# The SSD output weight's first half kept in the dead columns of the normalised input

## The chip, the cores and the metric

The kernel runs on one core of one Trainium2 chip. The metric is the device time of one execution in microseconds (us), and the number that stands for a kernel is the median of several executions. A second number is used for the working: the span of one profiled execution, from its first to its last instruction.

## The reference, cut to what matters

One inference step of a two-layer decoder trunk. Layer 0 is a Mamba-2 state space mixer (SSD), layer 1 is latent attention (MLA); 1024 prompt tokens and 8 x 8 sample tokens use the same weights. Only the end of layer 0 matters here:

```python
y = y.reshape(b, t, SSD_D_INNER) * jax.nn.silu(z.astype(F32))
yg = y.reshape(b, t, SSD_GROUPS, SSD_D_INNER // SSD_GROUPS)
yg = yg * lax.rsqrt(jnp.mean(yg * yg, axis=-1, keepdims=True) + NORM_EPS)
y = yg.reshape(b, t, SSD_D_INNER) * norm_w.astype(F32)
out = jnp.einsum('bte,ed->btd', y.astype(h.dtype), w_out)
```

`z` is the gate: the normalised input times the first 2048 columns of `ssd_w_in`. `w_out` is 2048 x 1024 in float32. The result is added to the input rows and becomes the input of layer 1.

## The kernel before, in words

Tokens come in nine tiles: eight of 128 prompt tokens and one of 64 sample tokens. The 32 SSD heads come in eight groups of four. Every float32 operand of a large product is held as two halves, `hi` (rounded to the matmul's input format) and `lo` (the rest), and a product is three matmuls: hi*hi, hi*lo, lo*hi. Making the halves is one ACT instruction (`hi`) and one DVE or POOL instruction (`lo`).

The normalised input lies transposed in `xh` and `xl`, `[128, 8, 1152]` and `[128, 8, 1088]`: partition is input channel, the middle index its block of 128, the last index the token. For each group g, `Group.steps` makes 21 steps: 12 projections of convolution channels (line 88), then `gates`, nine steps, one for each token tile i, in which `mm_tok` (line 100) projects tile i with the columns `i*128 : i*128+128` of `xh` and `xl` as weights (tile names `pz`, then ACT copies the result to `z`, line 514). The scan of group g (`ssd_scan`, 13 pieces) is interleaved with the steps of group g+1. PSUM tiles tagged `pj` (two buffers) carry all projections.

After the steps of the last group 7, `left.close()` frees the pools on the left side of the on-chip memory (`wp` with the input weights, `rp`, `xT` with `xh` and `xl`, `al`). Only then `load_wout` (lines 709 to 720) brings in the first eight 128-row blocks of `w_out` into new tiles `woh` and `wol`: a 512 KB DMA into `wraw` (two buffers), an ACT instruction that multiplies with the norm weight and rounds (line 718), a DVE instruction for the rest (line 719). They lie where the freed pools were. Then the scan of group 7 runs, interleaved with pass "a" of `ssd_outproj`: for each token tile a load of four groups' rows (`yta`, line 734), a scaling on DVE (line 736), eight PE transposes (`ytpa`, line 746), their halves (`yha`, `yla`), and two half tiles of 24 matmuls each of 512 columns (`poa`, line 100), added to `xra` on DVE (line 755). The number of pieces of pass "a" that have been made after a weight `w` of the scan's 21 is `int((w - CA) * PAR)`, at most 17, with `CA = 4` and `PAR = 0.7`. What is left of the 18 pieces comes after the scan, beside the load of the second eight blocks; then comes pass "b" (`pob`) with them, then layer 1, whose first gate weights (`wgh`, `wgl`) and `ckv` weights (`ck0h` to `ck7l`) are loaded while pass "b" runs.

The program's text does not fix the order on each engine: at build time a scheduler orders the instructions of each engine, and each DMA queue, from a modelled timeline. On the chip every engine executes its own list strictly in that order, each instruction after waiting for what it needs. Almost all DMAs are issued by SP, in one such list.

Of the kernel before, what the change touches and what calls it, by code (L numbers as in the profile page):

```python
# [8 lines left out]
F32 = mybir.dt.float32  # L9
F32R = mybir.dt.float32r  # L10
AF = mybir.ActivationFunctionType
ALU = mybir.AluOpType
# [41 lines left out]
WORD = (0, 4, 6, 1, 2, 3, 5, 7)  # L54
NWA = 8
NR0 = 13
CA = 4
PAR = 0.7
YHB = {"ya": 2, "yb": 1}
XDB = 2  # L60
YB = 2
# [29 lines left out]
def mm_tok(nc, p, m, n, terms):  # L91
    ops = []
    for j, (a, b, a2, wh, wl) in enumerate(terms):
        if m == 64:
            x = [(p[:64, :n], a, wl), (p[:, :n], a2, wh)]
            ops += x if j else x[::-1]
        else:
            ops += [(p[:m, :n], *ab) for ab in ((a, wh), (a, wl), (b, wh))]
    for j, (o, a, b) in enumerate(ops):
        nc.tensor.matmul(o, a, b, start=(j == 0), stop=(j == len(ops) - 1))  # L100
        yield
# [604 lines left out]
    return load  # L706


def load_wout(k, pool, raws, kks, ws):
    nc = k.nc  # L710
    wo = k.I["ssd_w_out"][0]
    for kk in kks:
        hi = pool.tile([128, D], F32R, name=f"woh{kk}")
        lo = pool.tile([128, D], F32R, name=f"wol{kk}")
        raw = load_raw(raws, 1, D)[:, 0]
        nc.sync.dma_start(raw, wo[kk * 128 : kk * 128 + 128])
        nw = k.ssdn[:, kk : kk + 1]
        nc.scalar.activation(hi, raw, AF.Copy, scale=nw)
        nc.vector.scalar_tensor_tensor(lo, raw, nw, hi.bitcast(F32), op0=ALU.mult, op1=ALU.subtract)
        ws.append((hi, lo))  # L720


def ssd_outproj(k, ypools, ws, psum, k0, load, order, tag):
    nc = k.nc
    nk = len(ws)
    g0, ng = k0 // 2, nk // 2
    rs = k.cs.tile([128, 9, ng], F32, name="yrs" + tag)
    rstd_of(k, rs, k.yssq[:, :, g0 : g0 + ng], 256)
    for j, i in enumerate(order):
        t0, m = TILES[i]  # L730
        yp = ypools[j]
        nb = YHB[yp.name]
        y = yp.tile([128, ng, 256], F32, tag="yt", name=f"yt{tag}{i}", bufs=1)
        nc.sync.dma_start(y[:m].rearrange("p g c -> p (g c)"),
                          k.y_d[t0 : t0 + m, k0 * 128 : (k0 + nk) * 128])
        nc.vector.tensor_tensor(y[:m], y[:m], rs[:m, i].unsqueeze(2).to_broadcast([m, ng, 256]), op=ALU.mult)
        xr = yp.tile([128, D], F32, tag="xr", name=f"xr{tag}{i}", bufs=nb)
        load(xr, i)
        yh = yp.tile([128, nk, 128], F32R, tag="yh", name=f"yh{tag}{i}", bufs=nb)
        yl = yp.tile([128, nk, 128], F32R, tag="yl", name=f"yl{tag}{i}", bufs=nb)  # L740
        yv = y.rearrange("p g c -> p (g c)")
        for q in range(nk // 4):
            p = psum.tile([128, 512], F32, tag="tr", name=f"ytp{tag}{i}{q}", bufs=PB["tr"])
            for a in range(4):
                b = q * 4 + a
                nc.tensor.transpose(p[:, a * 128 : a * 128 + m], yv[:m, b * 128 : b * 128 + 128], k.ident[:m, :m])
            pv = p.rearrange("p (a t) -> p a t", a=4)[:, :, :m]
            qs = slice(q * 4, q * 4 + 4)
            split(k, yh[:, qs, :m], yh[:, qs, 64:] if m == 64 else yl[:, qs], pv)
        for hf in range(2):  # L750
            c = slice(hf * 512, hf * 512 + 512)
            p = psum.tile([128, 512], F32, tag="pj", name=f"po{tag}{i}{hf}", bufs=PB["pj"])
            drain(mm_tok(nc, p, m, 512, [(yh[:, kk, :m], yl[:, kk], yh[:, kk], ws[kk][0][:, c], ws[kk][1][:, c])
                                         for kk in range(nk)]))
            nc.vector.tensor_tensor(xr[:m, c], xr[:m, c], p[:m], op=ALU.add)
            if m == 64:
                nc.vector.tensor_tensor(xr[:m, c], xr[:m, c], p[64:], op=ALU.add)
            if hf == 0:
                yield
        (nc.gpsimd if k0 and i > 6 else nc.sync).dma_start(k.h_d[t0 : t0 + m], xr[:m])  # L760
        yield
# [6 lines left out]
def layer_ssd(k):  # L768
    tc, nc = k.tc, k.nc
    k.h0 = ExitStack()  # L770
    PB.update(PB1)
    stc = ExitStack()
    k.cs = stc.enter_context(open_pool(tc, name="cs", bufs=1))
    ssd_tiles(k)
    k.y_d = k.dram.tile([T, DIN], F32, name="y_d")
    k.h_d = k.dram.tile([T, D], F32, name="h_d")
    with ExitStack() as st:
        psum = st.enter_context(open_pool(tc, name="ps1", bufs=2, space=PS))
        left, right = ExitStack(), ExitStack()
        wp = left.enter_context(open_pool(tc, name="wp", bufs=2))  # L780
        rp = left.enter_context(open_pool(tc, name="rp", bufs=2))
        xp = left.enter_context(open_pool(tc, name="xT", bufs=1))
        k.xh = xp.tile([128, 8, T + 64], F32R, name="xh")
        k.xl = xp.tile([128, 8, T], F32R, name="xl")
        al = left.enter_context(open_pool(tc, name="al", bufs=1))
        gp = right.enter_context(open_pool(tc, name="gp", bufs=1, side="right"))
        pools = (wp, rp, gp, psum, (al, gp))
        g0 = Group(k, 0, pools)
        st0 = g0.steps()
        with open_pool(tc, name="x0", bufs=1, side="right") as p0:  # L790
            g0.raws[1] = p0

            k.sqp = lambda name: gp.tile([128, 5, 256], F32, tag="z", name=name, bufs=3).rearrange(
                "p a c -> p (a c)")[:, :D]

            def before():
                load_vectors(k, p0, psum)
                for bi in range(2):
                    g0.pre[bi] = g0.weights(bi)

            def after():
                ssd_consts(k)
                conv_state_T(k, p0, psum)

            norm_steps(k, x_loader(k), None, k.xh, k.xl, p0, psum, [st0], XB, before, after)
        for _ in range(6):
            next(st0)
        with open_pool(tc, name="zd", bufs=1, side="right") as p0:
            load_zdt(k, p0)
            for _ in st0:  # L810
                pass
            ssd_dt(k, p0, psum)
        sp = right.enter_context(open_pool(tc, name="sp", bufs=2, side="right"))
        k.cblk = [sp.tile([128, 4, 64], F32R, name=f"cblk{q}") for q in range(2)]
        for t in k.cblk:
            nc.gpsimd.memset(t.bitcast(F32), 0.0)
        gr = g0
        for g in range(G - 1):
            nx = Group(k, g + 1, pools)
            steps = nx.steps()  # L820
            done = 0
            w = 0
            for x in ssd_scan(k, gr, (sp, psum)):
                w += x
                while done < int(w + 0.01):
                    next(steps, None)
                    done += 1
            for _ in steps:
                pass
            gr = nx  # L830
        left.close()
        wsa, wsb = [], []
        wa = st.enter_context(open_pool(tc, name="woa", bufs=1))
        ya = st.enter_context(open_pool(tc, name="ya", bufs=1))
        load_wout(k, wa, wa, range(NWA), wsa)
        pa = ssd_outproj(k, (ya,) * 9, wsa, psum, 0, x_loader(k), range(9), "a")
        w, done = 0, 0
        for x in ssd_scan(k, gr, (sp, psum)):
            w += x
            while done < min(int((w - CA) * PAR), 17):  # L840
                next(pa)
                done += 1
        right.close()
        h0 = k.h0.enter_context(open_pool(tc, name="h0", bufs=1, side="right"))
        k.h0p = h0
        k.xt0 = [h0.tile([128, D], F32, tag="xt", name=f"xt{j}", bufs=3) for j in range(3)]
        k.sqp = lambda name: k.tok.rearrange("p i a h -> p (i a h)")[:, :D]
        yb = st.enter_context(open_pool(tc, name="yb", bufs=1, side="right"))
        wb = st.enter_context(open_pool(tc, name="wob", bufs=1, side="right"))
        load_wout(k, wb, wa, range(NWA, 16), wsb)  # L850
        for _ in pa:
            pass
        for j, _ in enumerate(ssd_outproj(k, YORD(yb, ya), wsb, psum, NWA, h_loader(k), range(9), "b")):
            if j == NR0:
                k.rows0 = norm_rows(k, 0, h_loader(k), h0, 3, k.xt0)
    stc.close()
# [452 lines left out]
def drain(g):  # L1309
    for _ in g:  # L1310
        pass
# [603 lines left out]
```

## Time and profile before

| what | us |
|---|---|
| median of three runs | 2028.72 (2023.08 to 2029.69) |
| the profiled execution, whole | 2021.9 |
| its span | 2020.1 |
| last gate projection on PE starts | 816.82 |
| first matmul of pass "a" starts | 835.35 |
| first matmul of pass "b" starts | 975.13 |

The page of the profile gives busy time by engine, the span in 40 slices (a digit is the busy share in tenths, and `PEclk` the granted TensorE clock in tenths of full speed), and groups of instructions. The views quoted below are: stretches of the span with each engine's busy time; the instructions of one engine in order of time (start, duration, engine, line, operation, tiles, count, and in brackets the idle time ahead of it with what ended it); and groups of equal instructions (line, engine, operation, tiles, shape, count | busy time, mean ns of one | idle time ahead).

### The profile page before, as it was taken

The numbers are of one execution on the slowest core, as the hardware profiler recorded it, in microseconds if no ns is written. First come the engines' busy times: TensorE is split into PE (matmuls) and PEld (weight loads), VectorE is DVE, ScalarE is ACT, GpSimd is POOL, SyncE is SP. The second block draws the span as 40 slices with busy tenths as digits, with TensorE's granted clock in tenths as the row PEclk, the third lists the DMA queues.
The fourth block names the chain that finished last, engine by engine and source line by source line (L and its number), as shares of the span: only waits on it lengthen the run. The fifth ranks groups of instructions, "written<-read, shape, count | busy, mean of one in ns | idle before, by whom it ended". The sixth has DMA issues, their size and how long they took to land. (4 is left out here: it accounts for less than half of the span.)

```text
span 2020.1 us, 33410 instructions
## 1 busy us (share of the span) xinstructions
PE 1920.7 (95%) x12001; PEld 1744.5 (86%) x12001; DVE 1223.7 (61%) x2459; ACT 1107.6 (55%) x2535; POOL 788.6 (39%) x979
## 2 busy tenths in 40 slices
PE   6999999999999999899998999999999999799998
PEld 5899999999999999787777998898888887688887
DVE  4547566656566666755334314567787877866675
ACT  5456667666666666632114314435676777655552
POOL 1327555555655545631000001103343334755551
PEclk9999999999999999799999999999999999999999
DMA  4213323332333332645534432232121112554541
GB/s 149 57 51 93 90 86 92 82 97 82 93 82 96 85 97 66 214 141 193 167 120 138 129 147 76 73 104 65 49 66 39 50 39 78 167 170 135 148 146 37
DMA packets 182461, 206.59 MB, mean 102 GB/s; under 512 B 18988, under 2 KB 147896, under 8 KB 181912
## 3 DMA queue, kind: packets, MB, share of 16 engines
q1 hardware_dynamic: 177240, 184.67, 30.7%
q0 software_dynamic: 4976, 19.66, 3.2%
q8 instruction: 95, 1.56, 0.3%
q14 instruction: 70, 0.57, 0.1%
q10 hardware_dynamic: 80, 0.13, 0.0%
HBM read 151.10 MB, written 53.28 MB: 101 GB/s over the span
## 5 line engine op out<-in xcount | busy, mean ns | idle before, releaser
L88 PE MATMUL pj<-xh,wih 128*128 128x384 f32 (+1 forms) x768 | 256.5, 338 | 9.5 <-ACT xh L239 5.2
L88 PE MATMUL pj<-xl,wih 128*128 128x384 f32 (+1 forms) x768 | 255.4, 333 | 0.0
L88 PE MATMUL pj<-xh,wil 128*128 128x384 f32 (+1 forms) x768 | 255.0, 332 | 0.0
L474 DVE SCALAR_TENSOR_TENSOR acc<-raw,vec,acc 128x1112 f32<-128x1112 f32 x96 | 141.5, 1478 | 25.5 <-ACT acc L471 24.6
L88 PEld LDWEIGHTS pj<-xh,wih 128*128 128x128 f32 x768 | 145.8, 191 | 11.8 <-ACT xh L239 6.2
L1274 POOL TENSOR_TENSOR tl<-P,th 128x384 fp32r<-128x384 f32 (+1 forms) x96 | 91.0, 948 | 164.9 <-ACT P L1272 134.8
L88 PEld LDWEIGHTS pj<-xl,wih 128*128 128x128 f32 x768 | 146.3, 191 | 0.9
L88 PEld LDWEIGHTS pj<-xh,wil 128*128 128x128 f32 x768 | 146.1, 190 | 0.4
L100 PE MATMUL pz<-wih,xh 128*128 128x256 f32 x504 | 142.5, 286 | 0.0
L100 PE MATMUL pz<-wil,xh 128*128 128x256 f32 (+1 forms) x504 | 140.2, 284 | 0.0
L1271 ACT ACTIVATE th<-st 128x512 fp32r<-128x512 f32 x192 | 94.2, 490 | 65.2 <-PE st L1267 42.8
L100 PE MATMUL pz<-wih,xl 128*128 128x256 f32 x448 | 128.3, 286 | 0.0
L577 ACT ACTIVATE M<-M,tok 128x128 f32<-128x128 f32 (+1 forms) x288 | 90.5, 386 | 66.7 <-DVE M L574 66.5
L1563 POOL TENSOR_TENSOR kvl<-pgr,kvh 128x1024 fp32r<-128x1024 f32 x32 | 78.2, 2445 | 66.9 <-ACT kvh L1562 66.9
L100 PEld LDWEIGHTS pz<-wih,xh 128*128 128x128 f32 x504 | 95.8, 190 | 0.3
L1272 ACT ACTIVATE P<-st 128x512 f32<-128x512 f32 x192 | 93.3, 486 | 0.0
L100 PEld LDWEIGHTS pz<-wil,xh 128*128 128x128 f32 (+1 forms) x504 | 92.7, 184 | 0.8
L574 DVE TENSOR_TENSOR M<-M,negu 128x512 f32<-128x512 f32 x64 | 50.6, 791 | 68.7 <-DMA M<-acs_d 68.4
L130 DVE TENSOR_TENSOR wil<-wraw,wih 128x512 fp32r<-128x512 f32 x88 | 72.3, 829 | 30.2 <-ACT wih L129 28.8
L100 PEld LDWEIGHTS pz<-wih,xl 128*128 128x128 f32 x448 | 85.2, 190 | 0.1
L1274 DVE TENSOR_TENSOR tl<-P,th 128x512 fp32r<-128x512 f32 x96 | 72.0, 750 | 21.3 <-ACT P L1272 21.1
L560 POOL TENSOR_TENSOR xdd<-xsT,tok 128x256 f32<-128x256 f32 x64 | 49.6, 775 | 73.0 <-ACT xsT L546 72.7
(818 smaller groups left out, 6327.3 us busy)
## 6 DMA issues: line engine op xcount, KB each, us to landing
wraw<-in_ssd_w_in SPq DMA_DIRECT2D x92, 256.0 KB
M<-acs_d SPq DMA_DIRECT2D x64, 256.0 KB
s<-in_state_ssm SPq DMA_DIRECT2D x32, 256.0 KB
y_d<-y SPq DMA_DIRECT2D x64, 128.0 KB
out_s_ssm<-s SPq DMA_DIRECT2D x32, 256.0 KB
wraw<-in_ssd_w_out SPq DMA_DIRECT2D x16, 512.0 KB
q_d<-qt SPq DMA_DIRECT2D x32, 192.0 KB
qp<-q_d SPq DMA_DIRECT2D x8, 768.0 KB
```

What stands on the lines that cost most here:

```text
L88: nc.tensor.matmul(out, a, b, start=(i == 0), stop=(i == n - 1))
L100: nc.tensor.matmul(o, a, b, start=(j == 0), stop=(j == len(ops) - 1))
L130: (eng or nc.vector).tensor_tensor(lo, src, hi.bitcast(F32), op=ALU.subtract)
L474: nc.vector.scalar_tensor_tensor(acc, raw[:, j : j + n], k.convw[j][:, blk : blk + 1], acc, op0=ALU.mult, op1=ALU.add)
L560: nc.gpsimd.tensor_tensor(v3(xdd), v3(xsT), hb(2), op=ALU.mult)
L574: nc.vector.tensor_tensor(M[:m, :, :m], M[:m, :, :m], (k.negs if smp else k.negu)[:m, :m].unsqueeze(1).to_broadcast([m, 4, m]), op=ALU.add)
L577: nc.scalar.activation(M[:m, h, :m], M[:m, h, :m], AF.Exp, bias=tk[:, 0, 4 * g + h : 4 * g + h + 1])
L1271: nc.scalar.activation(th[:, :n], ps[:, :n], AF.Exp, scale=SCALE)
L1272: nc.scalar.activation(P[:, :n], ps[:, :n], AF.Exp, scale=SCALE)
L1274: eng.tensor_tensor(tl[:, :n], P[:, :n], th[:, :n].bitcast(F32), op=ALU.subtract)
L1563: nc.gpsimd.tensor_tensor(rl, raw, rh.bitcast(F32), op=ALU.subtract)
```

## The change: what it does, and the diff

Three edits belong together. The first eight blocks of `w_out` get no tiles of their own: block kk's halves are written into columns `kk*128 : kk*128+128` of all eight channel blocks of `xh` and `xl` (`wout_cols`), 8 x 128 values in each partition, and read from there as 4 x 128 columns by the matmuls of pass "a". Token tile kk's columns are dead once the last group's gate projection of tile kk is done. So `last_steps` issues blocks 0 to 3 inside the steps of group 7, ahead of steps 13, 15, 17 and 19 (gate projections of tiles 1, 3, 5 and 7 by index), with `rp`'s `raw` buffers for the raw rows; blocks 4 to 7 follow after `left.close()` with two raw buffers in a new small pool `wor`. Pool `xT` moves out of the group of pools that `left.close()` frees, so `xh` and `xl` stay, and all pools that are opened later lie elsewhere than before. `CA` goes from 4 to 1 and `PAR` from 0.7 to 0.6, so pass "a" starts earlier in the scan, at a lower rate: int(17 x 0.7) = 11 pieces within the scan before, int(20 x 0.6) = 12 now. The buffer that holds the descriptors of DMAs issued by POOL (the page gathers of layer 1 above all) is set to 4096 bytes.

```diff
-CA = 4
-PAR = 0.7
+CA = 1
+PAR = 0.6
+WCOLS = (13, 15, 17, 19)
...
+def wout_halves(k, kk, raw, hi, lo):
+    nc = k.nc
+    nw = k.ssdn[:, kk : kk + 1]
+    nc.scalar.activation(hi, raw, AF.Copy, scale=nw)
+    nc.vector.scalar_tensor_tensor(lo, raw, nw, hi.bitcast(F32), op0=ALU.mult, op1=ALU.subtract)
+
+
+def wout_cols(k, kk, raw, ws):
+    k.nc.sync.dma_start(raw, k.I["ssd_w_out"][0][kk * 128 : kk * 128 + 128])
+    cs = slice(kk * 128, kk * 128 + 128)
+    hi, lo = k.xh[:, :, cs], k.xl[:, :, cs]
+    wout_halves(k, kk, raw.rearrange("p (k e) -> p k e", k=8), hi, lo)
+    ws.append((hi, lo))
+
+
+def last_steps(k, steps, rp, ws):
+    for n, _ in enumerate(steps):
+        if n in WCOLS:
+            kk = len(ws)
+            wout_cols(k, kk, rp.tile([128, RAW], F32, tag="raw", name=f"wor{kk}", bufs=2)[:, :D], ws)
+        yield
...
-            drain(mm_tok(nc, p, m, 512, [(yh[:, kk, :m], yl[:, kk], yh[:, kk], ws[kk][0][:, c], ws[kk][1][:, c])
-                                         for kk in range(nk)]))
+            p4 = p.rearrange("p (a e) -> p a e", a=4)
+            drain(mm_tok(nc, p4, m, 4, [(yh[:, kk, :m], yl[:, kk], yh[:, kk], ws[kk][0][:, b4], ws[kk][1][:, b4])
+                                        for kk in range(nk)]))
...
+        xp = st.enter_context(open_pool(tc, name="xT", bufs=1))
         wp = left.enter_context(open_pool(tc, name="wp", bufs=2))
         rp = left.enter_context(open_pool(tc, name="rp", bufs=2))
-        xp = left.enter_context(open_pool(tc, name="xT", bufs=1))
...
+        wsa, wsb = [], []
         for g in range(G - 1):
             nx = Group(k, g + 1, pools)
-            steps = nx.steps()
+            steps = nx.steps() if g < G - 2 else last_steps(k, nx.steps(), rp, wsa)
...
         left.close()
-        wsa, wsb = [], []
-        wa = st.enter_context(open_pool(tc, name="woa", bufs=1))
+        wr = st.enter_context(open_pool(tc, name="wor", bufs=1))
         ya = st.enter_context(open_pool(tc, name="ya", bufs=1))
-        load_wout(k, wa, wa, range(NWA), wsa)
+        for kk in range(len(wsa), NWA):
+            wout_cols(k, kk, load_raw(wr, 1, D)[:, 0], wsa)
...
-    nc = bacc.Bacc("TRN2", target_bir_lowering=False, num_devices=1)
+    nc = bacc.Bacc("TRN2", target_bir_lowering=False, num_devices=1, dynamic_dma_scratch_size=4096)
```

**ACT, in the last gate projections.** `xs` and `M` belong to the convolution and the scan, `z` is a gate result, `wor` is a raw block of `w_out`. Before:

```order
L436 ACTIVATE xs_9836<-acc_9416 128x128
L514 COPY z_9876<-pz 128x256
L577 ACT_TABLE_LOAD
L577 ACTIVATE M_7_10121<-M_7_10121,tok 128x128 x4
L604 ACTIVATE xD_5_9796,yssq<-y_5_9823 128x256
```

The change, from the same instruction on:

```order
L437 ACTIVATE xs_9836<-acc_9416 128x128
L713 ACTIVATE xh<-wor_9929,vec 128x8x128
L515 COPY z_9876<-pz 128x256
L713 ACTIVATE xh<-wor_10043,vec 128x8x128
L605 ACTIVATE xD_5_9796,yssq<-y_5_9823 128x256
L130 COPY Ch_7_10117<-acc_7707 128x128
```

The rounding of two blocks now stands around a gate copy, and the exponentials of `M_7` with their table load come later; two more blocks follow in the same way further down.

**PE, after the last gate projection.** `pv`, `trp`, `sn`, `cb`, `st` and `py` belong to the scan of group 7, `ytpa` are the transposes of pass "a" and `poa` its matmuls. Before:

```order
L666 MATMUL pv_800_10422<-sh_800_10418,cblk_1098 64x128
L541 MATMUL trp_1_10438<-ident,acc_9416 128x128
...
L541 MATMUL trp_2_10496<-ident,acc_9416 128x128
...
L673 MATMUL sn_800_10434<-bb_80_10409,x_80_10403 128x512
L571 MATMUL cb_1_10464<-acc_9019 128x128
L746 MATMUL ytpa_10564<-ident,yta_10557 128x128 x4
L88 MATMUL st_1_10479<-xddh_1_10450,BTh_1_10444 128x256
L746 MATMUL ytpa_10571<-ident,yta_10557 128x128 x4
...
L100 MATMUL poa_10578<-woh_10296,yha_10562 128x512
```

The change, from the last `pv` on:

```order
L667 MATMUL pv_800_10405<-sh_800_10401,cblk_1098 64x128
L766 MATMUL ytpa_10431<-ident,yta_10424 128x128 x4
L766 MATMUL ytpa_10438<-ident,yta_10424 128x128 x4
L101 MATMUL poa_10445<-xh,yha_10429 128x512
L101 MATMUL poa_10445<-xl,yha_10429 128x512
L101 MATMUL poa_10529<-xh,yha_10429 128x512
L101 MATMUL poa_10529<-xl,yha_10429 128x512
L674 MATMUL sn_800_10417<-bb_80_10392,x_80_10386 128x512
L572 MATMUL cb_1_10497<-acc_9019 128x128
L101 MATMUL poa_10445<-xh,yla_10430 128x512
```

The transposes and the first matmuls of pass "a" now stand ahead of `trp`, `sn`, `cb` and `st` of the scan's next tiles.

**DVE, at the seam of the two layers.** `xrb` are the last additions of pass "b", `hl` is the low half of layer 1's normalised input. Before:

```order
L755 TENSOR_TENSOR xrb_12307<-xrb_12307,pob_12344 64x512
L757 TENSOR_TENSOR xrb_12307<-xrb_12307,pob_12344 64x512
L130 TENSOR_TENSOR wgl<-wraw,wgh 128x1024 x2
L130 TENSOR_TENSOR ck0l<-wraw,ck0h 128x288
L130 TENSOR_TENSOR ck1l<-wraw,ck1h 128x288
L240 TENSOR_SCALAR hl<-xtp_0_12400,vec,hh 128x384
```

The change:

```order
L131 TENSOR_TENSOR wgl<-wraw,wgh 128x1024 x2
L777 TENSOR_TENSOR xrb_12290<-xrb_12290,pob_12308 64x512
L779 TENSOR_TENSOR xrb_12290<-xrb_12290,pob_12308 64x512
L777 TENSOR_TENSOR xrb_12290<-xrb_12290,pob_12327 64x512
L131 TENSOR_TENSOR ck0l<-wraw,ck0h 128x288
L131 TENSOR_TENSOR ck1l<-wraw,ck1h 128x288
L779 TENSOR_TENSOR xrb_12290<-xrb_12290,pob_12327 64x512
L131 TENSOR_TENSOR wgl<-wraw,wgh 128x1024
L241 TENSOR_SCALAR hl<-xtp_0_12384,vec,hh 128x384
```

The first two `wgl` now stand ahead of the last additions of pass "b", and a third one stands between those and the first `hl`.

More of the change, by code (lines that the diff above doesn't have):

```diff
@@ L706, in h_loader @@
     return load
+def wout_halves(k, kk, raw, hi, lo):
[15 more added lines that the diff above has]
+        yield
 def load_wout(k, pool, raws, kks, ws):
-    nc = k.nc
-    wo = k.I["ssd_w_out"][0]
     for kk in kks:
-        hi = pool.tile([128, D], F32R, name=f"woh{kk}")
-        lo = pool.tile([128, D], F32R, name=f"wol{kk}")
+        hi = pool.tile([128, 8, 128], F32R, name=f"woh{kk}")
+        lo = pool.tile([128, 8, 128], F32R, name=f"wol{kk}")
         raw = load_raw(raws, 1, D)[:, 0]
[L716 to L719, printed above, removed]
+        k.nc.sync.dma_start(raw, k.I["ssd_w_out"][0][kk * 128 : kk * 128 + 128])
+        wout_halves(k, kk, raw.rearrange("p (k e) -> p k e", k=8), hi, lo)
         ws.append((hi, lo))
@@ L751, in ssd_outproj @@
             c = slice(hf * 512, hf * 512 + 512)
+            b4 = slice(hf * 4, hf * 4 + 4)
             p = psum.tile([128, 512], F32, tag="pj", name=f"po{tag}{i}{hf}", bufs=PB["pj"])
-            drain(mm_tok(nc, p, m, 512, [(yh[:, kk, :m], yl[:, kk], yh[:, kk], ws[kk][0][:, c], ws[kk][1][:, c])
-                                         for kk in range(nk)]))
+            p4 = p.rearrange("p (a e) -> p a e", a=4)
+            drain(mm_tok(nc, p4, m, 4, [(yh[:, kk, :m], yl[:, kk], yh[:, kk], ws[kk][0][:, b4], ws[kk][1][:, b4])
+                                        for kk in range(nk)]))
             nc.vector.tensor_tensor(xr[:m, c], xr[:m, c], p[:m], op=ALU.add)
@@ L849, in layer_ssd @@
         wb = st.enter_context(open_pool(tc, name="wob", bufs=1, side="right"))
-        load_wout(k, wb, wa, range(NWA, 16), wsb)
+        load_wout(k, wb, wr, range(NWA, 16), wsb)
         for _ in pa:
```

## The prediction, put down before the changed kernel ran

> **What bounds the kernel now.** I read the page first: the busy times, and the slices of PE and of its clock.
>
> ```profile
> PE 1920.7 (95%) x12001; PEld 1744.5 (86%) x12001; DVE 1223.7 (61%) x2459; ACT 1107.6 (55%) x2535; POOL 788.6 (39%) x979
> ...
> PE   6999999999999999899998999999999999799998
> ...
> PEclk9999999999999999799999999999999999999999
> ```
>
> PE is busy for 95% of the span, so a change can only win what PE loses: idle time, and time at the lower clock. The one dip of the clock is slice 17 (808 to 858 us), the place of the change: the last gate projections end there and pass "a" begins. So the next view is this stretch in pieces. The columns are the stretch, its length, PE, PEld, DVE, ACT and POOL busy, the granted clock, the DMA engines' share and GB/s.
>
> ```profile
> 816.50:820.00 3.50, 2.32 (x21) 1.72 (x18) 2.04 (x5) 3.43 (x10) 1.36 (x4) 1.00 0.33 102
> 820.00:823.50 3.50, 3.04 (x13) 2.64 (x13) 1.76 (x5) 3.47 (x7) 1.41 (x3) 0.55 0.95 349
> 823.50:827.00 3.50, 1.68 (x7) 1.26 (x8) 3.41 (x6) 2.40 (x7) 2.82 (x3) 0.50 1.00 377
> 827.00:830.50 3.50, 2.76 (x14) 1.90 (x12) 3.47 (x4) 2.17 (x9) 2.64 (x3) 0.50 0.83 317
> 830.50:834.00 3.50, 2.95 (x12) 2.28 (x11) 3.50 (x8) 3.47 (x8) 3.50 (x5) 0.50 0.57 172
> 834.00:837.50 3.50, 2.75 (x9) 2.36 (x10) 2.58 (x5) 3.50 (x8) 2.66 (x4) 0.50 0.81 241
> 837.50:841.00 3.50, 3.50 (x16) 3.26 (x16) 3.28 (x5) 1.51 (x4) 2.08 (x4) 0.53 0.72 235
> 841.00:861.50 20.50, 17.85 (x113) 14.80 (x111) 18.46 (x28) 12.49 (x31) 15.08 (x18) 1.00 0.74 236
> ```
>
> Busy time multiplied by clock is PE's work at full rate: 2.3 + 1.7 + 0.8 + 1.4 + 1.5 + 1.4 + 1.9 = 11.0 of the 24.5 us up to 841, then 17.9 of 20.5. The stretch loses 13.5 + 2.6 = 16.1 us, 0.8% of the span. That is the ceiling here. DVE is full from 823.5 to 834 and the DMA engines from 820 to 827.
>
> **The first term: the start of pass "a".** Next, the instructions of PE, DVE and ACT in order of time (PE, then DVE from 826.75, then ACT from 830.80).
>
> ```profile
> 816.82 0.28 PE L100 MATMUL pz<-wih,xh 128*128 128x256 f32 x1
> 827.40 0.31 PE L666 MATMUL pv<-sh,cblk 128*64 128x128 f32 x1
> 831.62 1.06 PE L746 MATMUL ytpa<-ident,yta 128*128 128x128 f32 x4
> 834.75 0.58 PE L88 MATMUL st<-xddl,BTh 128*128 128x256 f32 x1 [0.79 <-POOL xddl L130]
> 835.35 0.63 PE L100 MATMUL poa<-woh,yha 128*128 128x512 f32 x1
> 856.09 0.50 PE L100 MATMUL poa<-wol,yha 128*128 128x512 f32 x1 [1.04 <-DVE wol L719]
> ...
> 826.75 0.42 DVE L603 TENSOR_TENSOR y<-y,z 128x256 f32<-128x256 f32 x1
> 827.09 2.06 DVE L736 TENSOR_TENSOR yta<-yta,yrsa 128x1024 f32<-128x1024 f32 x1
> 829.52 1.27 DVE L719 SCALAR_TENSOR_TENSOR wol<-wraw,vec,woh 128x1024 fp32r<-128x1024 f32 x1
> ...
> 830.80 1.28 ACT L577 ACT_TABLE_LOAD   x1
> 832.10 1.28 ACT L577 ACTIVATE M<-M,tok 128x128 f32<-128x128 f32 x4
> 833.28 0.56 ACT L129 CAST yha<-ytpa 128x512 fp32r<-128x512 f32 x1
> ```
>
> The weights are not what the first `poa` waits for: it needs `yha`, which stands on ACT behind a table load and four exponentials, and the transposes, which stand on PE behind `trp`, `sn` and `cb`. The changed order takes away both. On DVE `yta` moves ahead of the `y*z` of 0.42 us, so it starts at about 826.75 and ends at 826.75 + 2.06 = 828.8. The transposes come straight behind `pv` (done at 827.7), so they wait for `yta` alone: 828.8, twice 1.06, end 830.9. `yha` follows the transposes at once, ahead of the table load. So the first `poa` starts at about 830.9 and not at 835.35. It has blocks 0 to 3 from the gate phase; 4 and 5 are done by DVE at about 824.5 and 830.5, as the first two are now.
>
> PE's loss after the change: up to 830.9 it does the work of the first four stretches, 6.2 us, less six `trp` and part of `sn` (-1.0), plus eight transposes at half rate (+1.0): 6.2 of 14.4, so 8.2 lost. From then on it has matmuls in stock, at the low clock at first. The clock came back 6.2 us after the last gap (834.75 to 841); 6.2 us from 830.9 cost another 3.1. Together 11.3 instead of 13.5. Of the 2.6 us lost after 841 the wait of 1.04 for `wol` goes and I let half of the rest go: 1.8. So -2.2 - 1.8 = **-4.0 us**. The ends: -1 (`yta` lands no earlier than DVE reaches it now, only the reordering on ACT counts) and -8 (half of the 16.1).
>
> [...]
>
> **The second term: the gate phase pays for it.** Four roundings on ACT of 1.15 us and four on DVE of 1.28 move from the scan of group 7 into the last gate projections, with four loads of 512 KB on SP's queue.
>
> ```profile
> 790.00:800.00 10.00, 10.00 (x87) 9.95 (x86) 6.91 (x13) 8.83 (x20) 6.55 (x10) 1.00 0.31 84
> 800.00:815.00 15.00, 14.82 (x125) 14.19 (x125) 5.69 (x13) 7.77 (x21) 5.80 (x9) 1.00 0.20 62
> ...
> 795.48 0.35 ACT L514 COPY z<-pz 128x256 f32<-128x256 f32 x1
> 799.65 0.36 ACT L514 COPY z<-pz 128x256 f32<-128x256 f32 x1
> ...
> 791.20 0.41 SPq L654 DMA_DIRECT2D s<-in_state_ssm  x1
> 817.79 0.88 SPq L716 DMA_DIRECT2D wraw<-in_ssd_w_out  x2
> 822.08 1.13 ACT L718 ACTIVATE woh<-wraw,vec 128x1024 fp32r<-128x1024 f32 x1
> ```
>
> From 800 to 815 ACT is free for 7.2 of 15 us and DVE for 9.3, so 4.6 and 5.1 us have room. The delicate part is the order: the rounding of block 0 stands ahead of a gate copy, and whatever ACT waits for, that copy and PE's `pj` buffer wait for too. The load is issued behind `s`, at about 792. A load of the same kind took 4.3 us from issue to use (817.79 to 822.08) with the DMA engines full; here their share is 0.2 to 0.31. So block 0 is there at 796.5 at the latest, the copy comes at 797.7 instead of 795.48, and PE wants the buffer at about 799.3, when it is done with the next tile. The cover is 1.6 us. I take **+0.5 us**, between nothing (all covered) and +4 (each of four roundings, 1.15, uncovered).
>
> **The third term: the seam of the layers.** DVE and PE again.
>
> ```profile
> 1084.46 2.35 DVE L130 TENSOR_TENSOR wgl<-wraw,wgh 128x1024 fp32r<-128x1024 f32 x2
> 1087.58 1.67 DVE L240 SCALAR_TENSOR_TENSOR hl<-xtp,vec,hh 128x384 fp32r<-128x384 f32 x3
> 1081.53 0.68 DVE L755 TENSOR_TENSOR xrb<-xrb,pob 64x512 f32<-64x512 f32 x1 [5.77 <-PE pob L100]
> 1088.25 0.90 PE L238 MATMUL xtp<-ident,xt 128*128 128x128 f32 x3 [2.97 <-DVE hl L240]
> ```
>
> PE waits 2.97 us for `hl`, which stands behind two `wgl` of 2.35 us. In the changed order these two lie ahead of the additions of pass "b", where DVE idles 5.77 us, and one other `wgl` (1.18) comes in their place, if its load is there. So `hl` comes 2.35 + 0.4 - 1.18 = 1.6 us earlier, and as the loads behind the freed buffers start earlier too, I take **-2.0 us**, between 0 (the third `wgl` is late) and -3 (the whole wait goes).
>
> **Edits taken as nothing.** The matmuls of pass "a" read 4 x 128 columns instead of 512 in a row, and the halves are written as 8 x 128. Rows with such patterns: the values' weights product reads 8 x 16 columns, beside a transpose that reads 128 in a row; and `cqh` is written as 4 x 128, `yhb` as 512 in a row.
>
> ```profile
> L1631 PE MATMUL lo<-accT,wv x32: 271/275/276, 1998.9 to 2002.3; 128*128 128x128 f32 x32
> L541 PE MATMUL trp<-ident,acc 128*128 128x128 f32 x64 | 17.9, 279 | 0.0
> L129 ACT CAST yhb<-ytpb 128x512 fp32r<-128x512 f32 x16 | 8.6, 589 | 60.0 <-PE ytpb L746 60.0
> L129 ACT CAST cqh<-cqs 128x512 fp32r<-128x512 f32 x8 | 4.9, 617 | 5.5 <-DVE cqs L1007 5.5
> L1486 POOL DMA_INDIRECT pgr<-in_cache_ckv,ptidx x32 | 37.4, 1168 | 8.6 <-POOL kvl L1563 6.6 <-issue 0.7 <-PE o L1293 0.3
> ```
>
> 275 ns stand against 279, so PE pays nothing from the nearer row; the far end, the 5% of ACT's 617 over 589, would be 416 x 0.229 x 0.05 = 4.8 us. The smaller buffer for POOL's descriptors could only make the 32 gathers wait; POOL waits 8.6 us ahead of them in all, mostly for its own `kvl`, and at most four are on the way at once. I take 0; the far end is one more issue time each, 37 us, and has 3% with me. The lower rate of pass "a" leaves six of its pieces instead of seven behind the scan; the second half of the weights had been ready long before it was used, so that is 0 too.
>
> **The sum.** -4.0 + 0.5 - 2.0 = -5.5 us from the rows; and as the scan of group 7 no longer shares DVE with eight `wol` (10 us of DVE time while it was full), about -1 more between 841 and 900: **-6.5 us**. The profiled execution took 2021.9 us around a span of 2020.1; it would take 2015.4. It lies 6.8 us under the median of the runs shown, so I put the same difference on the median: 2028.72 - 6.5 = **2022.2 us**.
>
> **Rivals.**
> 1. *The wait only moves* (25%): `yta` lands behind 1.5 MB of other loads in the full DMA stretch 820 to 827, PE starts pass "a" with two pieces and stalls again for blocks 6 and 7. For it: DVE's order sets `yta`, and its neighbours did not move. Against it: DVE was not waiting for `yta` at 827.09. Time: -1 - 1 = -2, 2026.7.
> 2. *Slower: ACT stuck behind a late block* (20%). In the gate phase ACT's list holds a rounding ahead of a gate copy four times. It decides from 1.6 us of lateness on; with loads 4 us later than I think each costs PE 2.4, and the clock drops as at 820, 3.4 us at half rate: 4 x 2.4 + 3.4 - 4 = +9, 2037.7. For it: four new places where two queues must meet, with 1.6 us of cover by my own estimate. Against it: the low DMA share there. The gathers' and the strided reads' far ends count here too (+4 to +30).
> 3. *More is won* (10%): the gap closes by half and the seam fully, -8 - 3 - 1 = -12, 2016.7.
>
> My forecast has 45%, with -4 to -9. About 0.3% (6.1 us) is what a measurement of this kernel can tell from no change. Of the forecast's case 0.38 lies beyond that, with rival 3 and 0.02 of rival 1 that makes faster 0.50; same 0.30, the rest of both; slower 0.20. The range: from rival 3, less the spread of the three runs' median downwards (2023.08 is 5.6 below it), 2011; up to 2038, rival 2's own time, which leaves out half of that rival, 0.1, and the low half of rival 3, 0.05.
>
> **What would show it.** Right: first `poa` at 829 to 833 after the last `pz`, the clock back one piece earlier, no `ACT` wait for `wor` over 1.5 us, matmuls of 387 to 389 ns in pass "a", `hl` at the seam without the 2.97. Wrong: PE idle at `pz` with the releaser `z`, a first `poa` at 835 behind `yta`, longer `poa`, POOL waiting at its gathers.

## The result: slower by 0.64%

The changed kernel took 2040.42 us in the median of six runs (2034.91 to 2044.77), the kernel before 2027.22 (2023.08 to 2029.69, six runs). The ratio is 1.0064, with a 95% interval of 1.0045 to 1.0083, so 13 us were lost. The prediction was 2022.2, with a range from 2011 to 2038.

The profiled execution of the changed kernel took 2043.3 us. Its page, the busy times and the slices of PE and of its clock:

```profile
PE 1927.2 (94%) x12001; PEld 1748.3 (86%) x12001; DVE 1227.7 (60%) x2459; ACT 1108.1 (54%) x2535; POOL 781.4 (38%) x979
...
PE   6999999999999999898998999999999999899998
...
PEclk9999999999999999899999999999999999999999
```

The dip of the clock in slice 17 is shallower than before (8 instead of 7), and the time is longer all the same. So the loss must be looked for stage by stage. I cut both traces at the same instructions: the last transpose of the conv state (`ctp`), the last `pz`, the first `poa`, the first `ytpb` of pass "b"; and for the seam from the last `pob` to the first `kpt`, the transposes of the page rows in layer 1. The stretches, first of the kernel before (columns as in the prediction):

```profile
785.37:816.82 31.45, 31.27 (x265) 30.60 (x262) 17.12 (x32) 20.47 (x49) 15.15 (x21) 1.00 0.23 67
816.82:835.35 18.53, 13.03 (x63) 10.07 (x62) 14.59 (x25) 15.98 (x38) 13.01 (x16) 0.59 0.75 262
835.35:970.62 135.27, 125.65 (x645) 102.45 (x645) 78.37 (x119) 46.92 (x111) 44.62 (x52) 0.97 0.53 171
1082.71:1126.30 43.59, 36.81 (x206) 32.03 (x205) 27.19 (x52) 24.81 (x48) 3.76 (x5) 0.92 0.61 191
```

And of the changed kernel:

```profile
791.08:825.07 33.99, 31.64 (x264) 30.75 (x262) 21.91 (x35) 25.33 (x53) 16.87 (x21) 1.00 0.39 123
825.07:838.25 13.18, 8.19 (x51) 6.20 (x49) 10.40 (x18) 9.51 (x24) 5.56 (x10) 0.74 0.89 302
838.25:982.65 144.40, 127.92 (x658) 104.88 (x658) 76.47 (x124) 48.64 (x120) 46.21 (x58) 0.95 0.47 152
1094.70:1143.36 48.66, 38.47 (x206) 31.34 (x205) 24.61 (x50) 24.61 (x48) 3.77 (x5) 0.93 0.52 163
```

The lengths tell it. The gate projections take 2.5 us more (33.99 against 31.45). The way to the first `poa` takes 5.4 less, as hoped. Then the rest of the scan and of pass "a" takes 9.1 more (144.40 against 135.27), and the seam 5.1 more. The sum is +11.3 us, and pass "b" between them is the same. What is left of the 21 us between the two spans lies outside: 5.7 us up to the gate projections and some 4 in layer 1; the repetition below (e1) shows that most of this comes and goes with no edit.

### The profile page after: what moved, and what is told of

Its sections match the earlier page's. It is cut to its first block, busy times and chain, and to the rows that moved or that the text cites. A ratio compares the mean times of both kernels' runs of the same rounds, so it can differ in the third digit from the quotient of the medians.

```text
span 2041.2 us, 33396 instructions
## 1 busy us (share of the span) xinstructions
PE 1927.2 (94%) x12001; PEld 1748.3 (86%) x12001; DVE 1227.7 (60%) x2459; ACT 1108.1 (54%) x2535; POOL 781.4 (38%) x979
## 5 line engine op out<-in xcount | busy, mean ns | idle before, releaser
L89 PEld LDWEIGHTS pj<-xh,wih 128*128 128x128 f32 x768 | 146.2, 191 | 12.6 <-ACT xh L240 6.5
L89 PEld LDWEIGHTS pj<-xl,wih 128*128 128x128 f32 x768 | 146.7, 191 | 0.9
L131 DVE TENSOR_TENSOR wil<-wraw,wih 128x512 fp32r<-128x512 f32 x88 | 71.9, 825 | 31.5 <-ACT wih L130 30.3
## 6 DMA issues: line engine op xcount, KB each, us to landing
q_d<-qt SPq DMA_DIRECT2D x32, 192.0 KB
```

Of the source, the lines that this page charges most:

```text
L89: nc.tensor.matmul(out, a, b, start=(i == 0), stop=(i == n - 1))
L131: (eng or nc.vector).tensor_tensor(lo, src, hi.bitcast(F32), op=ALU.subtract)
```

## The experiments

All kernels were timed against the kernel before in five rounds. For each, the trace was cut in the same way. "To pass b" is the stretch from the last `ctp` to the first `ytpb`, and the two columns behind it are parts of it.

| kernel | CA, PAR | ratio (95%) | to pass b | gate | last pz to first poa | seam |
|---|---|---|---|---|---|---|
| before | 4, 0.7 | 1 | 185.2 | 31.5 | 18.5 | 43.6 |
| changed | 1, 0.6 | 1.0064 (1.0045-1.0083) | 191.6 | 34.0 | 13.2 | 48.7 |
| e1 changed again | 1, 0.6 | 1.0056 (1.0036-1.0076) | 192.0 | 33.9 | 13.1 | 48.7 |
| e2 page table first | 1, 0.6 | 1.0037 (1.0017-1.0056) | 191.9 | 33.8 | 13.1 | 43.5 |
| e3 old rate | 4, 0.7 | 1.0022 (1.0004-1.0040) | 184.6 | 34.1 | 17.5 | 45.8 |
| e4 before, new rate | 1, 0.6 | 1.0061 (1.0039-1.0083) | 197.8 | 31.8 | 14.6 | 43.6 |
| e5 e2 + old rate | 4, 0.7 | 1.0030 (1.0013-1.0047) | 180.6 | 33.9 | 17.4 | 46.6 |
| e6 e2, PAR 0.7 | 1, 0.7 | 0.9998 (0.9984-1.0012) | 184.4 | 33.6 | 13.3 | 41.6 |
| e7 e2, CA 4 | 4, 0.6 | 1.0058 (1.0037-1.0080) | 191.8 | 33.9 | 17.4 | 44.4 |
| e8 e5, no early block | 4, 0.7 | 0.9998 (0.9982-1.0014) | 186.2 | 31.5 | 18.5 | 45.4 |
| e9 before, small buffer | 4, 0.7 | 1.0010 (0.9995-1.0025) | 182.2 | 31.5 | 18.2 | 43.7 |
| e10 e2, CA 2 | 2, 0.75 | 1.0008 (0.9996-1.0021) | 184.2 | 33.5 | 13.5 | 45.4 |
| e11 before, CA 1 | 1, 0.7 | 1.0017 (1.0001-1.0032) | 187.0 | 31.8 | 14.6 | 43.9 |
| e12 e2, PAR 0.8 | 1, 0.8 | 1.0033 (1.0019-1.0046) | 188.4 | 33.7 | 14.1 | 47.8 |

**e1, the changed kernel again.** No edit. My theory at this point had three parts: the rate of pass "a" costs in the scan, the order at the seam costs there, and the rest is chance. The rivals were that the early roundings cost, and that the moved buffers cost everywhere.

> The changed kernel once more, unedited. If the profiled execution of it was unlucky outside the change, the loss of PE up to the gate phase (41.2 us against 36.1 of before) and from the seam to the end (the loss after the seam was about 24 us in the weights-and-heads stretch against 19) differs by several us in this profile; if the moved buffers or the smaller descriptor buffer cost there, both come back within 1 us. The ratio to before stays at 1.0045 to 1.0083 either way, and the wait for the page table (DVE 7.3 us, PE 4.8 us at the seam) comes back if it is a matter of order and not of chance.

The stage lengths came back within 0.6 us, the gate, the way to pass "b" and the seam. The part ahead of the gate projections took 784.6 us instead of 791.1, and PE's loss there, idle time and lower clock together, was about 35 instead of about 41. So these 6 us were chance. The wait for the page table was there again, 5.46 us on DVE.

**e2, the page table ahead of the gather.** The wait is in these rows of the changed kernel (SP, POOL, DVE, PE):

```profile
1117.75 0.43 SPq L1392 DMA_DIRECT2D kpidx<-in_page_table  x1
1121.96 0.33 SPq L1416 DMA_DIRECT2D ptab<-in_page_table  x1
...
1121.06 1.17 POOL L1394 DMA_INDIRECT kprows<-in_cache_kpe,kpidx  x1 [2.28 <-PE xtp L239]
...
1130.56 0.75 DVE L1422 CAST ptf<-ptab 32x32 f32<-32x32 int32 x4 [7.26 <-DMA ptab<-in_page_table]
...
1132.32 1.90 PE L239 MATMUL xtp<-ident,xt 128*128 128x128 f32 x6 [4.79 <-DVE hl L241]
```

The page table `ptab` is issued 0.9 us behind a gather of 2.1 MB, and its first reader starts 8.6 us later, 0.3 us after the gather has landed (9.2 us from its issue). DVE has its cast ahead of `hl`, and PE waits 4.79 us for `hl`. In the kernel before the order was the other way round:

```profile
1111.94 0.33 SPq L1393 DMA_DIRECT2D ptab<-in_page_table  x1
...
1114.43 1.17 POOL L1371 DMA_INDIRECT kprows<-in_cache_kpe,kpidx  x1 [4.06 <-DMA kpidx<-in_page_table]
...
1115.04 0.92 DVE L1399 CAST ptf<-ptab 32x32 f32<-32x32 int32 x4 [0.45 <-DMA ptab<-in_page_table]
```

There `ptab` went out 2.5 us ahead of the gather, and DVE waited 0.45 us. SP held `ptab` back in the changed kernel: it waited 3.9 us for the PE transposes `xtp`, which read the tile whose place `ptab` takes. The edit puts it ahead in the queue:

```diff
             gk = gather_kpe(k, kg)
-            next(gk)
             page_rows(k, kg)
+            next(gk)
```

> The page table's load is put ahead of the page indices' load, so that it no longer waits for a PE transpose and lands before the gather fills the DMA engines; nothing else moves. Theory A (the seam is lost to this queue order): PE's wait of 4.79 us for hl behind the page table goes, the seam is 3 to 6 us shorter, the ratio to before is 0.002 to 0.003 lower than that of the changed kernel. Rival (the wait moves to the next late hh or hl, or the gather that now comes later makes the later rows late): the seam is shorter by less than 1.5 us, same ratio within 0.001.

The seam fell from 48.7 to 43.5 us, the length of before. In e2 `ptab` goes out 4.9 us ahead of the gather, and no wait stands ahead of the cast:

```profile
1112.47 0.42 SPq L1416 DMA_DIRECT2D ptab<-in_page_table  x1
...
1117.41 1.17 POOL L1394 DMA_INDIRECT kprows<-in_cache_kpe,kpidx  x1 [3.92 <-PE xtp L239]
...
1119.36 0.75 DVE L1422 CAST ptf<-ptab 32x32 f32<-32x32 int32 x4
```

In the profile theory A holds: the late page table was what PE waited for. The times point the same way (0.0019 lower than e1), but their intervals overlap.

Being behind the gather is not enough, though. In e3, e4, e9 and e11, which keep the old lines, `ptab` goes out 0.2 to 5.6 us behind the gather, DVE waits 1.7 to 2.9 us for it, and PE waits for `hl` behind it about 1 us at most. The row of e9, whose gather went out at 1106.09 and `ptab` at 1110.40:

```profile
1114.65 0.76 DVE L1399 CAST ptf<-ptab 32x32 f32<-32x32 int32 x4 [2.90 <-DMA ptab<-in_page_table]
```

What it costs may depend on how early DVE comes to the cast, and on what PE has left to do then; no run tests that. Nor does the exchange set the length of the seam by itself: in the kernels that have it the seam takes from 41.6 to 47.8 us.

**e3 and e4, the rate alone, from both sides.** e3 takes the new rate out of the changed kernel, e4 puts it into the kernel before:

```diff
-CA = 1
-PAR = 0.6
+CA = 4
+PAR = 0.7
```

> The changed kernel with CA = 4 and PAR = 0.7 again, so that pass a starts later in the scan and at the old rate; the weights still go into the input's columns. Theory R (the new rate loses what the earlier start won, since it leaves late steps of the scan uncovered): PE's loss from the last gate projection to the first transposes of pass b falls from 29 us by 4 to 8 us, ratio 1.001 to 1.004. Rival T (the early roundings and loads in the gate phase, and the order that the scheduler makes of them, are what costs): the loss stays within 2 us, ratio as the changed kernel's within 0.0015. Rival U (the earlier start is worth what was predicted): it gets 3 to 6 us worse, ratio 1.008 to 1.010.

> The kernel before with only CA = 1 and PAR = 0.6; the weights stay in their own tiles after the gate phase. Theory R: slower than before by 4 to 8 us, ratio 1.002 to 1.004, with new waits of PE in the second half of the scan (for M, sl or xddh). Rival T: no change, ratio 0.999 to 1.001. Rival U (the earlier start helps by itself): ratio 0.997 to 0.999.

Theory R held in both, in e4 beyond its range. e3 comes down to 1.0022, and its way to pass "b" to 184.6 us. e4, which differs from the kernel before in two numbers, is as slow as the whole change: 1.0061, 12 us, where I had expected 4 to 8. Its way to pass "b" is 12.6 us longer. Why is seen at one step of the scan. In the changed kernel PE (in order of time):

```profile
888.05 0.60 PE L658 MATMUL s0p<-ident,s 128*128 128x128 f32 x4
889.33 0.27 PE L667 MATMUL pv<-sh,cblk 128*64 128x128 f32 x1 [0.68 <-ACT sh L130]
891.82 0.31 PE L667 MATMUL pv<-sl,cblk 128*32 128x128 f32 x2 [2.23 <-DVE sl L131]
```

The scan's own chain goes from PE (`s0p`) to ACT (`sh`) and DVE (`sl`) and back to PE (`pv`). Between the two PE instructions nothing else is in the list, so PE waits 2.9 us. The same step in e3:

```profile
882.00 0.60 PE L658 MATMUL s0p<-ident,s 128*128 128x128 f32 x4
882.36 0.48 PE L101 MATMUL poa<-xh,yla 128*128 128x512 f32 x1
...
886.83 0.31 PE L667 MATMUL pv<-sl,cblk 128*32 128x128 f32 x2
```

Here 16 matmuls of pass "a" stand between them, and there is no wait at all. e4 has gaps like those of the changed kernel, one step after the other:

```profile
890.61 0.31 PE L666 MATMUL pv<-sl,cblk 128*32 128x128 f32 x2 [2.16 <-DVE sl L130]
910.03 1.10 PE L582 MATMUL py<-xsT,M 128*128 128x64 f32 x8 [1.58 <-ACT xsT L546]
927.63 1.08 PE L582 MATMUL py<-xsT,M 128*128 128x64 f32 x8 [0.92 <-DVE M L578]
930.62 0.44 PE L609 MATMUL pf<-ident,S 128*128 128x128 f32 x2 [0.70 <-DVE S L594]
```

**e6 and e7, which of the two numbers.** Both on top of e2, first e6, then e7:

```diff
-PAR = 0.6
+PAR = 0.7
```

```diff
-CA = 1
+CA = 4
```

> As e2 but with PAR = 0.7, CA stays 1. Theory P (the spacing of the pieces loses the time: at 0.6 the scan's waits find no matmuls in stock): the stretch to pass b falls from 192 to 187 or less, ratio 1.000 or less. Theory C (the early start, CA = 1, loses it: the pieces spent early are missing late): it stays at 190 or more, ratio 1.003 to 1.005.

> As e2 but with CA = 4, PAR stays 0.6: nine pieces in the scan and nine behind it. Theory P: the stretch to pass b stays at 189 us or more, ratio 1.002 to 1.005, with the waits of PE for M, sl and xsT in the second half of the scan. Theory C: 186 or less, ratio 0.999 to 1.001.

Of the two numbers it is `PAR` alone. With 0.6 the way to pass "b" took 191.6 to 192.0 us in four profiles with the weights in the columns, whatever `CA` was, and 184.6, 180.6, 184.4 and 186.2 with 0.7. The waits for `sl` (2.23), `xsT` (1.39), `M` (0.92) and `S` (0.70) from the middle of the scan on are in e7 as well, and in e6 they are gone. The early start does no harm, but it also gains nothing by the time pass "b" begins: from the last `pz` to the first `ytpb` e6 takes 150.8 us, e3 and e5 with the old `CA` 150.5 and 146.7, the kernel before and e9, which is the same program up to there, 153.8 and 150.7. e6 is the best of the versions with early blocks, and level with the kernel before.

**e5, both repairs.** e2 with the old rate:

```diff
-CA = 1
-PAR = 0.6
+CA = 4
+PAR = 0.7
```

> The two repairs together: page table first, and CA = 4 with PAR = 0.7; the weights still in the input's columns. If the effects of e2 and e3 add up, the stretch from the last conv transposes to the first transposes of pass b takes 184 to 185 us (185.2 in the kernel before), the seam 43 to 44 (43.6 before), ratio 0.997 to 1.000. If the seam's gain needs the late end of pass a (the rival: another wait appears with the old rate, as the seam of e3 already was 45.8), the seam stays over 45, ratio 1.001 to 1.003.

This did not add up. The way to pass "b" was even shorter than expected, 180.6 us, but the seam was 46.6, with a wait of 3.41 us for `ck2l` at its start, and the time was 1.0030. That is the rival's range. The same wait is in e3 (3.27 us), e7 (3.25) and e12 (4.00), so it is not `PAR` that brings it. In this profile layer 1 behind the seam was 9 us longer than in the kernel before, with a wait of 3.95 us that e6 does not have. No edit lies there. Most of the 9 us are clock (last section). Why all executions of e5 together were slower stays open.

**e8, no block in the gate phase.** On top of e5:

```diff
-WCOLS = (13, 15, 17, 19)
+WCOLS = ()
```

> As e5, but none of the eight blocks is rounded within the gate projections (WCOLS empty): all eight go into the input's columns after them. If the early blocks cost what the gate phase shows (2.3 us of PE against 0.2) and buy little, the gate phase is 2 us shorter, the way from the last gate projection to the first poa not over 1 us longer, ratio 0.002 or less below e5. If they buy the earlier start (first poa 17.5 us behind the last pz in e3, 18.5 in the kernel before), the two cancel, and the ratio is within 0.001 of e5.

The gate projections were back at 31.5 us, 2.4 shorter. The first `poa` came 1.1 us later after the last `pz`, and the ratio was 0.0032 below e5's. This fits "cost and buy little". But the way to pass "b" was longer than in e5, 186.2 against 180.6, and part of the difference in time lies in layer 1. e3, which is the same program as e5 up to the seam, took 184.6. So single stretches scatter by about 4 us, and the balance of the early blocks at this rate stays open within that.

**e9, the small descriptor buffer alone**, in the kernel before:

```diff
-    nc = bacc.Bacc("TRN2", target_bir_lowering=False, num_devices=1)
+    nc = bacc.Bacc("TRN2", target_bir_lowering=False, num_devices=1, dynamic_dma_scratch_size=4096)
```

> The kernel before with only the descriptor buffer of 4096 bytes. [...] Rival L (it costs in layer 1): POOL waits over 12 us there, layer 1 from the seam on 4 us longer or more, ratio 1.002 or more.

Nothing that can be measured: 1.0010, with an interval around 1. The group of POOL's gathers, of e9 and of the changed kernel:

```profile
L1486 POOL DMA_INDIRECT pgr<-in_cache_ckv,ptidx x32 | 36.4, 1139 | 9.1 <-POOL kvl L1563 6.8 <-issue 0.7 <-PE st L1267 0.3
```

```profile
L1509 POOL DMA_INDIRECT pgr<-in_cache_ckv,ptidx x32 | 37.4, 1169 | 9.2 <-POOL kvl L1586 6.8 <-issue 0.6 <-POOL tl L1297 0.3
```

It was 37.4 and 8.6 us before. Up to pass "b" e9 has the instructions of the kernel before in the same order, and its way there took 182.2 us instead of 185.2: chance again. At the seam the order differs: with this one edit two `wgl` stand ahead of the last additions of pass "b" and a third behind them, as in the changed kernel. PE's wait for the first `hl` falls from 2.97 us as it did there, and the seam takes 43.7 us all the same (43.6 before):

```profile
1085.51 0.85 PE L238 MATMUL xtp<-ident,xt 128*128 128x128 f32 x3 [1.11 <-DVE hl L240]
```

**e10 to e12, how far closer spacing goes.** e10 on top of e6, e11 on the kernel before, e12 on top of e6:

```diff
-CA = 1
-PAR = 0.7
+CA = 2
+PAR = 0.75
```

```diff
-CA = 4
+CA = 1
```

```diff
-PAR = 0.7
+PAR = 0.8
```

> As e6 but CA = 2 and PAR = 0.75: 14 pieces in the scan, four behind it. Theory P going on (closer pieces cover more): the stretch to pass b takes 181 to 184 us (184.4 in e6), ratio 0.997 to 0.999. Rival E (four pieces, 22 us, are fewer than the load of the second half needs): PE's loss behind the scan grows from 9 to 12 us or more, the stretch 185 or more, ratio 1.000 or more.

> The kernel before with only CA = 1: pass a starts early at the old spacing, the weights in tiles of their own. Theory P (the spacing alone lost the time in e4): the stretch to pass b is 185 to 188 us, not e4's 198, ratio 0.998 to 1.002. Rival W (without early weights an early start waits for wol, as in e4 with 1.2 and 2.2 us): 189 or more, ratio 1.002 or more, with waits of PE for wol of over 3 us in all.

> As e6 but PAR = 0.8: 16 pieces in the scan, two behind it. Rival E here surely: two pieces, 11 us, can't cover the load of eight blocks, which took 21 us behind the scan before; PE's loss behind the scan 12 to 18 us, less what the scan's loss falls (at most 3): the stretch to pass b 187 to 195, ratio 1.002 to 1.005. If theory P went on even here: 184 or less, ratio under 1.000.

The gain ends at 0.7. e10 was level with e6 on the way (184.2), between the theory and the rival, and with 0.75 the wait that 0.7 had removed is back:

```profile
886.20 0.31 PE L667 MATMUL pv<-sl,cblk 128*32 128x128 f32 x2 [2.23 <-DVE sl L131]
```

So closer spacing does not cover the scan's chains in every case. e12 took 188.4 us and 1.0033, the rival's range, but not for the rival's reason: of PE's time, 10.5 us are lost in the scan (6.1 in e6), and behind it 7.6 (9.7 in e6) and not 12 to 18. Some 3 us more go behind the stretch, where the first `pob` waits.

e11 shows what the early blocks do buy where pass "a" starts early. Without them PE waits for `wol` twice, 1.22 and 2.02 us, and the way is 187.0 us instead of 184.4. That is inside the scatter, but the two waits are plain, and e4 had them too (1.23 and 2.19).

## Why the prediction was wrong, step by step

1. **The start of pass "a": right at the first `poa`, but it did not last.** Forecast was a first `poa` 14.1 us after the last `pz` (830.9 less 816.82); it was 13.2. The rows of the changed kernel:

```profile
825.07 0.28 PE L101 MATMUL pz<-wih,xh 128*128 128x256 f32 x1
836.49 1.94 PE L766 MATMUL ytpa<-ident,yta 128*128 128x128 f32 x8 [0.24 <-PE pv L667]
838.25 0.79 PE L101 MATMUL poa<-xh,yha 128*128 128x512 f32 x1
...
835.16 1.23 DVE L756 TENSOR_TENSOR yta<-yta,yrsa 128x1024 f32<-128x1024 f32 x1
```

`yta`, transposes and `yha` follow one another as forecast. That the weights are not what it waits for was right too, further than I said: the four early blocks brought the start forward by 1.1 us (e8 against e5), and `CA = 1` by 4.1 (e5 against e6).

PE's loss up to the first `poa` fell from 11.0 us to 7.2. The sum took that as won. The wait of 1.04 us for `wol` went as well, but a longer one came in its neighbourhood, in each of the kernels with early blocks, `CA = 1` and 0.6 or 0.7. In the changed kernel:

```profile
856.62 1.08 PE L583 MATMUL py<-xsT,M 128*128 128x64 f32 x8 [2.17 <-DVE M L579]
```

2. **"The lower rate of pass a leaves six of its pieces instead of seven behind the scan ... so that is 0 too": this step failed.** I counted the pieces and asked only whether the weights would be late. I did not ask what the pieces did inside the scan. There they are the stock from which PE fills the scan's own chains. How little separates the two rates can be counted with the kernel's own rule. The scan is made in 13 steps, each with the weight 21/13. With 0.6 every step from the first one that has any is followed by one piece. With 0.7 it is the same, but one step in the middle (the seventh with `CA = 4`, the sixth with `CA = 1`, and there the last one too) is followed by two. In the last six steps the kernel before and the changed one get one piece each time. So what 0.6 lacks there is one piece of 24 matmuls in stock, and not a higher rate. That this one piece is the whole cause is a reading; no run moved it alone.

The trace of before could have told me that the scan needs cover. From 860 us to the scan's end at 922 it has one wait of PE over 0.4 us, at the same chain that cost 2.23 us above, and something must have covered the others:

```profile
906.75 0.31 PE L666 MATMUL pv<-sl,cblk 128*32 128x128 f32 x2 [0.88 <-DVE sl L130]
```

The gain of 5.4 us became a loss of 3.8 by the start of pass "b" (157.6 against 153.8 us from the last `pz`). PE's loss in the three parts of this way, idle time and lower clock together, worked out from each trace:

| kernel | CA, PAR | last pz to first poa | to the scan's end | to pass b |
|---|---|---|---|---|
| before | 4, 0.7 | 11.0 | 7.1 | 7.0 |
| e9 | 4, 0.7 | 10.6 | 5.4 | 5.5 |
| e3 | 4, 0.7 | 10.2 | 4.4 | 7.3 |
| e5 | 4, 0.7 | 10.2 | 3.6 | 4.6 |
| changed | 1, 0.6 | 7.2 | 11.9 | 9.7 |
| e2 | 1, 0.6 | 7.2 | 13.0 | 8.9 |
| e6 | 1, 0.7 | 7.3 | 6.1 | 9.7 |

The rate costs in the scan, as e2 and e6 show. Behind the scan they lose alike, and more than the kernels with `CA = 4` and 0.7: much of what the early start wins goes there. So the other half of the forecast's sentence, on the second half of the weights, falls short too. These weights are not late for their own use, but the roundings of their blocks wait on ACT for the loads, and `yha` stands behind them. In the changed kernel (ACT, then PE), and the longest such wait before (PE):

```profile
962.46 1.15 ACT L713 ACTIVATE woh<-wraw,vec 128x1024 fp32r<-128x1024 f32 x1 [1.64 <-DMA wraw<-in_ssd_w_out]
963.51 1.05 ACT L130 CAST yha<-ytpa 128x512 fp32r<-128x512 f32 x2
...
964.13 0.80 PE L101 MATMUL poa<-xh,yha 128*128 128x512 f32 x1 [5.41 <-ACT yha L130]
```

```profile
937.30 0.50 PE L100 MATMUL poa<-woh,yha 128*128 128x512 f32 x1 [2.44 <-ACT yha L129]
```

With `CA = 1` the step from 0.7 to 0.6 costs 7.5 us on the way to pass "b" with the weights in the columns (191.9 in e2, 184.4 in e6), and 10.8 with tiles of their own (197.8 in e4, 187.0 in e11).

3. **The seam: wrong in sign.** Forecast -2.0; it was +5.1. What I foresaw happened: the two `wgl` moved, and PE's wait for the first `hl` fell from 2.97 to 1.09 us.

```profile
1090.54 2.36 DVE L131 TENSOR_TENSOR wgl<-wraw,wgh 128x1024 fp32r<-128x1024 f32 x2 [2.80 <-DMA h_d<-xrb]
1099.11 0.55 PE L239 MATMUL xtp<-ident,xt 128*128 128x128 f32 x3 [1.09 <-DVE hl L241]
```

But that is worth nothing to the seam, as e9 shows, which has this order and the length of before. And I followed the moved loads only to the instruction that I wanted to come earlier, and not the ones behind them in SP's list. The page table came late behind the gather, 20 us further on. e2 shows it, since this one exchange brings the seam back to 43.5 us.

4. **The gate phase: the mechanism right, the size too small.** Forecast +0.5, between 0 and +4; it was +2.5, and +2.4 by e8. The first rounding came as worked out, 11.4 us behind the last `ctp` (forecast 11.1: 796.5 less 785.37). The waits came further on (ACT, then PE):

```profile
802.46 1.15 ACT L713 ACTIVATE xh<-wor,vec 128x1024 fp32r<-128x1024 f32 x1 [1.18 <-DMA wor<-in_ssd_w_out]
803.52 0.35 ACT L515 COPY z<-pz 128x256 f32<-128x256 f32 x1
809.14 0.35 ACT L515 COPY z<-pz 128x256 f32<-128x256 f32 x1
...
809.54 0.39 PE L101 MATMUL pz<-wih,xh 128*128 128x256 f32 x1 [1.11 <-ACT z L515]
```

The load took the 4.3 us that I had taken, from 798.16. The late copy is a later one, at 809.14, which stands behind two roundings, a table load and four exponentials. Another 1.22 us went at the next `cb`, which waited for a copy (`yo`) behind two more roundings. I had looked at the first of the four places only. Rival 2 was this mechanism, but with a late block as its cause and 9 us as its price. No run shows the 3.4 us at half rate of its sum in this phase: the granted clock was 1.00 from 791.08 to 825.07, with the wait of 1.11 us at `pz` in it, and the drop at 820 in the kernel before, which it names, lasted 20.5 us.

5. **The edits taken as nothing: right but for the rate.** The matmuls of pass "a" with the strided columns, before and changed:

```profile
L100 PE MATMUL poa<-wol,yha 128*128 128x512 f32 x128 | 51.5, 403 | 1.2 <-DVE wol L719 1.0
```

```profile
L101 PE MATMUL poa<-xl,yha 128*128 128x512 f32 x128 | 51.6, 403 | 0.0
```

403 ns both times. The descriptor buffer cost nothing that can be measured (e9), but this edit alone brings the changed order at the seam.

## What to carry to other kernels

- When two streams share an in-order engine, the rate of the filler is not only a matter of how many pieces are left at the end. Look at the longest chain of the other stream and count the filler instructions that stand inside it; where there are none, the engine waits: here 2.9 us with none between `s0p` and `pv`, and not at all with 16.
- Time won at the start of a stretch is not won until its end. Follow it to the next stage: here an earlier start by 4 to 5 us was gone at pass "b".
- Follow a moved load past the instruction that it helps, to what stands behind it in its queue. Here a small load behind a gather of 2.1 MB was there only at the gather's end, and PE waited 4.8 us; in four other kernels PE waited about 1 us or less.
- An edit of two constants beside a large rearrangement deserves its own line in the sum and its own run.

## What the hardware showed that was not expected

The same wait does not cost the same. In layer 1 PE waits 1.85 us for `wt` in the kernel before and in e5 alike. The kernel before, the wait and the clock in the 7 us behind it:

```profile
1633.34 0.66 PE L1206 MATMUL ql12p<-qsn,wt 64*128 64x64 f32 x4 [1.85 <-ACT wt L1202]
...
1633.50:1640.50 7.00, 7.00 (x47) 6.51 (x48) 4.36 (x13) 4.77 (x12) 1.56 (x2) 1.00 0.02 4
```

The same in e5:

```profile
1631.53 1.11 PE L1229 MATMUL ql12p<-qsn,wt 64*128 64x64 f32 x4 [1.85 <-ACT wt L1225]
...
1631.50:1638.50 7.00, 6.97 (x28) 6.53 (x28) 2.02 (x7) 2.22 (x5) 0.10 (x1) 0.52 0.02 4
```

In one the clock stayed at 1.00, in the other it was at 0.52 for 7 us, which costs 3.4 us of work. What decides between the two is shown by no run. Layer 1 has four such places between 1375 and 1695, three gaps of 1.8 us and one of 4.3. In the kernel before alone, the three equal gaps went with 3.4, 6.8 and 0 us at half clock. PE's loss to the clock over this stretch was about 7 us in the profile of before, 12 in that of the changed kernel, 8 in its repetition, 13 in e5 and 4 in e6. So two profiles of one program can differ by 5 us there, and a sum made against one profile carries that.
